# Small fp32 products of a hybrid decoder kernel issued to parts of the TensorE array

## The chip, the cores and the metric

The kernel runs on one core of one Trainium2 chip. The metric is the device time of one execution in microseconds (us). Each kernel is timed over several runs, and one further execution is recorded by the hardware profiler. PE is TensorE's multiplying side and PEld its weight-loading side, DVE is VectorE, ACT is ScalarE, POOL is GpSimd, and SP is the engine that here only issues DMAs.

## What is computed

The reference is a two-layer causal decoder trunk on 512 tokens of width 1024, all in float32. Cut to its frame:

```python
for layer in range(2):
    hn = _rmsnorm(h, norm_mix[layer])
    if layer == 0:
        proj = hn @ mix_w_in
        oa = _s5_mixer(proj[..., :512], ...)        # 32 groups of 16 channels, 64 complex states each
        ob = _hgrn2_mixer(proj[..., 512:], ...)     # 4 heads, chunked gated linear recurrence
        mix = concatenate([oa, ob], -1) @ mix_w_out
    else:
        mix = _dilated_attention(hn, positions, att_w_qkv, att_w_o)
    h = h + mix
    h = h + _conv_ffn(_rmsnorm(h, norm_ffn[layer]), ...)   # 1024 -> 2*2816, width-3 conv, gate, -> 1024
return _rmsnorm(h, norm_final)

# attention: 3 branches (dilation 1, 4, 16) x 8 heads of 64 dims, banded blocks of 128 queries
s = einsum('bdhnqe,bdhnke->bdhnqk', qb, kc)
o = einsum('bdhnqk,bdhnke->bdhnqe', exp(s - m), vc) / den      # then merged over the branches by their den
```

## The kernel before

Channels lie on the 128 partitions and the 512 tokens on the free axis. Every large product (projections, FFN, output projections) is made in three products of rounded parts: `mm3` (L183 to L187) multiplies the high and low parts of weights and activations into one PSUM bank of 512 columns. Weights stream from HBM in pieces of 1 MB, and ACT and DVE split each into `whi` and `wlo` (L124, L125). These products make up most of the program on TensorE. Between them stand many small products of plain fp32, whose operands are not split. In the trace each plain fp32 product stands as two weight loads and two matmuls, called two passes below.

The small products that the change touches are these:

- `rms_cols` (L258): the mean of squares of 128 tokens. The stationary operand is a 128x128 block of squares, the moving one a column of 1/1024. It runs four to eight times at each norm. For the attention's norm, four of the eight blocks take every fourth token (`"p (i r) -> p r i", r=4`).
- `s5_data` (L791, L811, L812): the S5 mixer in four feature tiles, 8 groups each. The first group of products takes 128x128 tables `gt` by 128x64 inputs `U`; then swap, multiplications and a scan on ACT, DVE and POOL make `X`; the second group adds `tz` by `U` and `ca` by `X` for each g. ACT copies the sum out (L814).
- `att_scores` (L1052, L1056): for a pair of heads e = 0, 1, which lie on partitions 0 to 63 and 64 to 127, blocks of 128 queries by 128 or 256 keys. Side 0 is the branch of dilation 1, with contiguous tokens. Side 1 is the two other branches, whose both operands take every fourth token.
- `att_merge` (L1140, L1142): probabilities, transposed to `pT`, by values, 64 columns of `v` for each head of the pair, into the banks `on` (side 0) and `oc` (side 1). Head e writes partitions 64e to 64e+63. DVE then multiplies both banks by the merge weights (L1146, L1147).

What else TensorE does between two large products is set by hand: `PROG` (L77) is text in which a dot stands for two or so large products and a letter for one step of a chain (`a`, `b`: S5; `h`, `k`: HGRN2; `s`: scores; `m`: merge). A chain's `yield` ends a step. A scheduler may move instructions a little, engine by engine; each engine then runs its own list in order.

Of the kernel before, what the change touches and what calls it, by code (L numbers as in the profile page):

```python
# [153 lines left out]
class Kernel:  # L154
# [94 lines left out]
    def rms_cols(self, blocks=(0, 1, 2, 3)):  # L249

        nc, ss = self.nc, self.ss
        u, n = blocks[0], len(blocks)
        pn = self.auxbank()
        parts = 1 if self.nsplit else 2
        for i in range(parts):
            for b in blocks:
                x = ss[i][:, 128 * b:128 * b + 128] if b < 4 else ss[i].rearrange("p (i r) -> p r i", r=4)[:, b - 4]
                nc.tensor.matmul(pn[:, b:b + 1], x, self.meanw, start=(i == 0 and b == u), stop=(i == parts - 1 and b == blocks[-1]))  # L258
        rc = self.xp.tile([128, 8], F32, name="rc")
        ms = self.xp.tile([128, 8], F32, name="ms")  # L260
        r = slice(u, u + n)
        nc.vector.tensor_scalar(ms[:, r], pn[:, r], EPS, None, op0=OP.add)
        self.rsqrt(rc[:, r], ms[:, r], self.xp, n)
        return rc
# [517 lines left out]
    def s5_data(self, ft, tables):  # L782
        nc = self.nc
        V, PL = nc.vector, nc.gpsimd
        gt, ca, tz, cs, sn, dec = tables
        U = self.U[ft]
        pa = self.auxbank()
        yield
        for g in range(8):
            o = slice(64 * g, 64 * g + 64)  # L790
            nc.tensor.matmul(pa[:, o], gt[:, g], U[:, g], start=True, stop=True)  # L791
        f = lambda ap: ap.rearrange("p g m -> p (g m)")
        z, t2, zs = self.tmp(), self.tmp(), self.tmp()
        self.swap(t2, pa)
        V.tensor_tensor(z, pa, f(cs), op=OP.mult)
        V.tensor_tensor(t2, t2, f(sn), op=OP.mult)
        V.tensor_tensor(z, z, t2, op=OP.add)
        V.tensor_tensor_scan(zs, f(dec), z, 0.0, op0=OP.mult, op1=OP.add)
        yield
        self.swap(t2, zs)  # L800
        X = self.tmp().rearrange("p (g m) -> p g m", g=8)
        PL.memset(X[:, :, 0:1], 0.0)
        z3 = lambda ap: ap.rearrange("p (g m) -> p g m", g=8)[:, :, 0:63]
        V.tensor_tensor(t2, t2, f(sn), op=OP.mult)
        PL.tensor_tensor(z, zs, f(cs), op=OP.mult)
        V.tensor_tensor(X[:, :, 1:64], z3(z), z3(t2), op=OP.subtract)
        yield
        py = self.auxbank()
        for g in range(8):
            o = py[:, 64 * g:64 * g + 64]  # L810
            nc.tensor.matmul(o, tz[:, g], U[:, g], start=True, stop=False)  # L811
            nc.tensor.matmul(o, ca[:, g, 2:10].rearrange("p d c -> p (d c)"), X[:, g], start=False, stop=True)  # L812
        ys = self.tmp()
        nc.scalar.activation(ys, py, AF.Copy)  # L814
        d = self.dr.tile([8, 128, 64], F32, name="yd")
        nc.scalar.dma_start(d.rearrange("i (c g) m -> (i c) (g m)", g=8), ys)
        yb = self.tmp()
        nc.scalar.dma_start(yb.rearrange("p (i m) -> p i m", i=8), d.rearrange("i p m -> p i m"))
        yield
        V.scalar_tensor_tensor(yb, self.u[:, ft], self.s5D[:, ft:ft + 1], yb, op0=OP.mult, op1=OP.add)  # L820
        nc.scalar.activation(self.u[:, ft], yb, AF.Gelu_apprx_tanh)
# [213 lines left out]
    def att_scores(self, side, pair):  # L1035


        nc, wk = self.nc, self.wk
        V, A, mm = nc.vector, nc.scalar, nc.tensor.matmul
        mx, st, qk = pair["mx"], pair["st"], pair["qk"]  # L1040
        k = 2 * side
        rows = [slice(64 * e, 64 * e + 64) for e in range(2)]
        p = [wk.tile([128, 4, 256], F32, name=f"p{side}", bufs=4) for e in range(2)]
        mask = self.mask[:, side:side + 2].rearrange("p a b -> p (a b)")
        for i in range(2):
            sc = [self.auxbank().rearrange("p (b n) -> p b n", b=2) for e in range(2)]
            for j in range(2):
                b = 2 * i + j
                c = 128 if side == 0 and b == 0 else 0
                for e, r in enumerate(rows):  # L1050
                    if side == 0:
                        mm(sc[e][:, j, c:], qk[0][r, 0, 128 * b:128 * b + 128], qk[0][r, 1, 128 * b - 128 + c:128 * b + 128], start=True, stop=True)  # L1052
                    else:
                        for g in (1, 2):
                            x = qk[g].rearrange("p a (i r) -> p a r i", r=4)
                            mm(sc[e][:, j, 128 * g - 128:128 * g], x[r, 0, b], x[r, 1, b], start=True, stop=True)  # L1056
            for e in range(2):
                for j in range(2):
                    b = 2 * i + j
                    c = 128 if side == 0 and b == 0 else 0  # L1060
                    V.tensor_tensor_reduce(p[e][:, b, c:], sc[e][:, j, c:], mask[:, c:], 1.0, NEG, OP.add, OP.max, accum_out=mx[:, e, b:b + 1])
                V.tensor_scalar(st[:, k, 2 * i:2 * i + 2, e], mx[:, e, 2 * i:2 * i + 2], -0.125, None, op0=OP.mult)
                for j in range(2):
                    b = 2 * i + j
                    c = 128 if side == 0 and b == 0 else 0
                    A.activation(p[e][:, b, c:], p[e][:, b, c:], AF.Exp, scale=0.125, bias=st[:, k, b, e:e + 1], accum_out=st[:, k, b, 2 + e:3 + e])
            if i == 0:
                yield
        for e in range(2):
            pair["p"][side, e] = p[e]  # L1070
        yield
# [42 lines left out]
    def att_merge(self, hp, pair):  # L1114
        nc, st = self.nc, pair["st"]
        V, mm = nc.vector, nc.tensor.matmul

        dc = self.dr.tile([T, 4], F32, name="dc")
        nc.sync.dma_start(dc.rearrange("(i r) n -> i r n", r=4), st[:, 2])
        nc.sync.dma_start(st[:, 1], dc.rearrange("(b p) n -> p b n", p=128))  # L1120
        yield
        pT = {}
        self.att_turn(pair, 1, 0, pT)
        yield
        W = self.att_weights(st)
        yield
        for side, e in ((0, 0), (1, 1), (0, 1)):
            self.att_turn(pair, side, e, pT)
            yield
        while None in [self.att_value(hp, g) for g in range(3)]:  # L1130
            yield
        vs = [self.att_value(hp, g) for g in range(3)]
        on, oc = self.auxbank(), self.auxbank()
        for e in range(2):
            s = slice(64 * e, 64 * e + 64)
            for b in range(4):
                hc = slice(128 * b, 128 * b + 128)
                todo = [j for j in range(2) if b or j]
                for j in todo:
                    mm(on[s, hc], vs[0][:, b - 1 + j, s], pT[0, e, b, j], start=(j == todo[0]), stop=(j == 1))  # L1140
                for j in range(2):
                    mm(oc[s, hc], vs[1 + j][:, b, s], pT[1, e, b, j], start=(j == 0), stop=(j == 1))  # L1142
            yield
        ot, o2 = (self.wk.tile([128, T], F32, name=n, bufs=1) for n in ("ot", "o2"))
        nat = lambda x: x.rearrange("p (i r) -> p r i", r=4)
        V.tensor_tensor(nat(o2), oc.rearrange("p (r i) -> p r i", r=4), nat(W[:, 1]), op=OP.mult)  # L1146
        V.tensor_tensor(ot, on, W[:, 0], op=OP.mult)  # L1147
        V.tensor_tensor(ot, ot, o2, op=OP.add)
        self.split(self.oh[:, hp], self.ol[:, hp], ot)
# [76 lines left out]
```

## Time and profile before

| | |
|---|---|
| median of 3 runs | 1317.2 us (1316.0 to 1318.52) |
| the profiled execution | 1316.5 us, span 1314.5 us |
| TensorE busy | 1271.3 us (97%), 6890 matmuls recorded |
| DVE busy | 821.9 us (63%) |
| ACT busy | 548.2 us (42%) |
| POOL busy | 144.4 us (11%) |
| mean granted TensorE clock | 0.988 |
| HBM traffic | 94 GB/s mean |

The span is the time between the first and the last instruction; the run's own time is 2.0 us longer. "Busy" is the share in which an engine has at least one instruction under way. Matmuls overlap one another in the array, so a matmul's recorded duration is longer than the step from one start to the next, and the steps are what adds up to time.

### The profile page before, as it was taken

The numbers are of one execution on the slowest core, as the hardware profiler recorded it, in microseconds if no ns is written. First come the engines' busy times: TensorE is split into PE (matmuls) and PEld (weight loads), VectorE is DVE, ScalarE is ACT, GpSimd is POOL, SyncE is SP. The second block draws the span as 40 slices with busy tenths as digits, with TensorE's granted clock in tenths as the row PEclk, the third lists the DMA queues.
The fourth block names the chain that finished last, engine by engine and source line by source line (L and its number), as shares of the span: only waits on it lengthen the run. The fifth ranks groups of instructions, "written<-read, shape, count | busy, mean of one in ns | idle before, by whom it ended". The sixth has DMA issues, their size and how long they took to land.

```text
span 1314.5 us, 17115 instructions
## 1 busy us (share of the span) xinstructions
PE 1271.3 (97%) x6890; PEld 1052.8 (80%) x6890; DVE 821.9 (63%) x1368; ACT 548.2 (42%) x867; POOL 144.4 (11%) x121
## 2 busy tenths in 40 slices
PE   7888999999999999999999999999899999999997
PEld 5677887878888888888888888898688888888886
DVE  7877688768777776333553535546777777773233
ACT  6457755335444444222334333424354444442221
POOL 2356111020000000001020101100300000000000
PEclk9989999999999999999999999999999999999998
DMA  6422122432223222222322322322122222222211
GB/s 208 136 69 77 49 81 59 136 101 94 96 96 100 97 97 96 96 97 96 109 82 92 94 96 73 94 81 81 62 97 98 100 96 96 96 96 96 97 64 65
DMA packets 36047, 123.19 MB, mean 94 GB/s; under 512 B 14912, under 2 KB 17536, under 8 KB 23296
## 3 DMA queue, kind: packets, MB, share of 16 engines
q1 hardware_dynamic: 22672, 113.32, 26.2%
q10 hardware_dynamic: 13296, 8.78, 2.3%
q8 instruction: 54, 0.88, 0.3%
q14 instruction: 25, 0.20, 0.1%
HBM read 116.26 MB, written 4.26 MB: 92 GB/s over the span
## 4 chain that ended last, share of the span: by engine, by line
PE 87%; DVE 8%; ACT 2%; issue 1%; POOL 1%; DMA 1%; ACTq 0%; DVEq 0%; SPq 0%; POOLq 0%
PE pt L185 26%; PE pt L187 26%; PE pt L186 26%; PE px L1056 1%; DVE wlo L125 1%; DVE xl L229 1%; PE px L1142 1%; PE px L1081 1%; PE px L1140 1%; PE px L812 1%; PE px L811 1%; PE px L517 1%; PE px L1052 1%; PE px L258 0%; DVE H L541 0%
## 5 line engine op out<-in xcount | busy, mean ns | idle before, releaser
L185 PE MATMUL pt<-xh,whi 128*128 128x512 f32 x1024 | 404.0, 395 | 8.9 <-ACT whi L124 7.1
L187 PE MATMUL pt<-xl,whi 128*128 128x512 f32 x1024 | 402.5, 393 | 2.3 <-DVE xl L229 2.3
L186 PE MATMUL pt<-xh,wlo 128*128 128x512 f32 x1024 | 401.9, 392 | 1.2 <-DVE wlo L125 1.2
L125 DVE TENSOR_TENSOR wlo<-stg,whi 128x1024 fp32r<-128x1024 f32 (+1 forms) x213 | 258.4, 1214 | 228.7 <-ACT whi L124 226.0
L124 ACT ACTIVATE whi<-stg 128x1024 fp32r<-128x1024 f32 (+1 forms) x213 | 215.7, 1013 | 261.7 <-PE pt L187 219.8
L185 PEld LDWEIGHTS pt<-xh,whi 128*128 128x128 f32 x1024 | 193.4, 189 | 51.7 <-ACT whi L124 7.5
L187 PEld LDWEIGHTS pt<-xl,whi 128*128 128x128 f32 x1024 | 193.7, 189 | 44.3 <-DVE xl L229 3.9
L186 PEld LDWEIGHTS pt<-xh,wlo 128*128 128x128 f32 x1024 | 193.9, 189 | 41.9 <-DVE wlo L125 2.3
L185 PE MATMUL pt<-ah,whi 128*128 128x512 f32 (+1 forms) x374 | 142.5, 381 | 0.0
L187 PE MATMUL pt<-al,whi 128*128 128x512 f32 (+1 forms) x374 | 141.7, 379 | 0.0
L186 PE MATMUL pt<-ah,wlo 128*128 128x512 f32 (+1 forms) x374 | 140.4, 375 | 0.0
L847 DVE TENSOR_TENSOR hu<-pt,rs 128x512 f32<-128x512 f32 x88 | 60.2, 688 | 62.8 <-PE pt L187 60.0
L187 PEld LDWEIGHTS pt<-al,whi 128*128 128x128 f32 x374 | 70.2, 188 | 14.5
L186 PEld LDWEIGHTS pt<-ah,wlo 128*128 128x128 f32 x374 | 70.2, 188 | 13.9
L185 PEld LDWEIGHTS pt<-ah,whi 128*128 128x128 f32 x374 | 70.3, 188 | 12.4
L848 ACT ACTIVATE b<-hu,cw 128x512 f32<-128x512 f32 x88 | 70.7, 808 | 5.0 <-DVE hu L847 4.4
L191 ACT ACTIVATE ah<-b 128x512 fp32r<-128x512 f32 x44 | 27.7, 630 | 107.3 <-DVE b L853 107.3
L237 POOL TENSOR_TENSOR ss<-H 128x512 f32<-128x512 f32 x4 | 4.5, 1135 | 595.0 <-DVE H L871 507.3
L850 DVE SCALAR_TENSOR_TENSOR b<-hu,cw,b 128x512 f32<-128x512 f32 x88 | 65.9, 751 | 2.7
L849 DVE SCALAR_TENSOR_TENSOR b<-hu,cw,b 128x512 f32<-128x512 f32 x88 | 65.5, 746 | 0.0
L852 ACT ACTIVATE b<-b 128x512 f32<-128x512 f32 x44 | 27.8, 632 | 72.9 <-DVE b L850 72.9
L185 PE MATMUL pt<-whi,xh 128*128 128x512 f32 x128 | 53.2, 415 | 0.0
(328 smaller groups left out, 1521.5 us busy)
## 6 DMA issues: line engine op xcount, KB each, us to landing
stg<-w_f SPq DMA_DIRECT2D x44, 1024.0 KB
stg<-w_g SPq DMA_DIRECT2D x22, 1024.0 KB
stg<-w_qkv SPq DMA_DIRECT2D x18, 1024.0 KB
stg<-w_mix SPq DMA_DIRECT2D x8, 1024.0 KB
H<-xT SPq DMA_DIRECT2D x8, 256.0 KB
stg<-w_moa SPq DMA_DIRECT2D x2, 1024.0 KB
b<-xT ACTq DMA_DIRECT2D x8, 256.0 KB
stg<-w_mob SPq DMA_DIRECT2D x2, 1024.0 KB
```

The costliest lines, as they stand in the source:

```text
L124: nc.scalar.activation(hi[:, c], s[:, c], AF.Copy)
L125: nc.vector.tensor_tensor(lo[:, c], s[:, c], hi[:, c].bitcast(F32), op=OP.subtract)
L185: mm(pt, sh, mh, start=first, stop=False)
L186: mm(pt, sl, mh, start=False, stop=False)
L187: mm(pt, sh, ml, start=False, stop=last)
L191: nc.scalar.activation(hi, x, AF.Copy)
L229: nc.vector.scalar_tensor_tensor(self.xl[:, i], x, g, self.xh[:, i].bitcast(F32), op0=OP.mult, op1=OP.subtract)
L847: V.tensor_tensor(x[:, 2:], pt, rs, op=OP.mult)
L848: nc.scalar.activation(y, x[:, 2:], AF.Identity, scale=cw[:, f, 2:3], bias=cw[:, f, 3:4])
L849: V.scalar_tensor_tensor(y, x[:, 1:T + 1], cw[:, f, 1:2], y, op0=OP.mult, op1=OP.add)
L850: V.scalar_tensor_tensor(y, x[:, 0:T], cw[:, f, 0:1], y, op0=OP.mult, op1=OP.add)
L852: nc.scalar.activation(half[0], half[0], AF.Silu)
```

## The change

Four kinds of small product are cut so that several of them occupy different parts of the array. The values of two heads (64 output columns each) alternate instead of one head following the other. A block of scores is cut into two halves of 64 queries, so that with the two heads there are four parts of 64 rows by 64 columns. The S5 products and the norms' column sums are cut into four parts of 32 output columns each. What is computed is the same, and the number of values multiplied too; there are more and smaller instructions. In `att_merge` the two steps now end after blocks 1 and 3 instead of after each head.

```diff
@@ rms_cols
-                nc.tensor.matmul(pn[:, b:b + 1], x, self.meanw, start=(i == 0 and b == u), ...)
+                for q in range(0, 128, 32):
+                    nc.tensor.matmul(pn[q:q + 32, b:b + 1], x[:, q:q + 32], self.meanw, start=(i == 0 and b == u), ...)
@@ s5_data
-            nc.tensor.matmul(pa[:, o], gt[:, g], U[:, g], start=True, stop=True)
+            for q in range(0, 128, 32):
+                nc.tensor.matmul(pa[q:q + 32, o], gt[:, g, q:q + 32], U[:, g], start=True, stop=True)
...
-            nc.tensor.matmul(o, tz[:, g], U[:, g], start=True, stop=False)
-            nc.tensor.matmul(o, ca[:, g, 2:10].rearrange("p d c -> p (d c)"), X[:, g], start=False, stop=True)
+            cx = ca[:, g, 2:10].rearrange("p d c -> p (d c)")
+            for y, z in ((tz[:, g], U[:, g]), (cx, X[:, g])):
+                for q in range(0, 128, 32):
+                    nc.tensor.matmul(py[q:q + 32, 64 * g:64 * g + 64], y[:, q:q + 32], z, start=(y is not cx), stop=(y is cx))
@@ att_scores
-                for e, r in enumerate(rows):
-                    if side == 0:
-                        mm(sc[e][:, j, c:], qk[0][r, 0, 128 * b:128 * b + 128], qk[0][r, 1, ...], start=True, stop=True)
-                    else:
-                        for g in (1, 2):
-                            mm(sc[e][:, j, 128 * g - 128:128 * g], x[r, 0, b], x[r, 1, b], start=True, stop=True)
+                for g in range(side, 2 * side + 1):
+                    for h in (slice(0, 64), slice(64, 128)):
+                        for e, r in enumerate(rows):
+                            if side == 0:
+                                mm(sc[e][h, j, c:], qk[0][r, 0, 128 * b:128 * b + 128][:, h], qk[0][r, 1, ...], start=True, stop=True)
+                            else:
+                                mm(sc[e][h, j, 128 * g - 128:128 * g], x[r, 0, b, h], x[r, 1, b], start=True, stop=True)
@@ att_merge
-        for e in range(2):
-            s = slice(64 * e, 64 * e + 64)
-            for b in range(4):
-                ...
-                    mm(on[s, hc], vs[0][:, b - 1 + j, s], pT[0, e, b, j], start=(j == todo[0]), stop=(j == 1))
-                    mm(oc[s, hc], vs[1 + j][:, b, s], pT[1, e, b, j], start=(j == 0), stop=(j == 1))
-            yield
+        for b in range(4):
+            todo = [(on, 0, j, vs[0][:, b - 1 + j]) for j in range(2) if b or j] + [(oc, 1, j, vs[1 + j][:, b]) for j in range(2)]
+            for po, side, j, v in todo:
+                for e in range(2):
+                    s = slice(64 * e, 64 * e + 64)
+                    mm(po[s, hc], v[:, s], pT[side, e, b, j], start=(j == 0 or side == 0 and b == 0), stop=(j == 1))
+            if b % 2:
+                yield
```

Three places show how the instructions stand on TensorE. A row gives line, operation, the tile written, the tiles read, output partitions by moving columns, and a count. The first is the values of the first pair of heads, head 0 before (its step is followed by head 1 later), where px_6165 is `on` and px_6166 is `oc`:

```order
L1140 MATMUL px_6165<-pT_5839,v0_5590 64x128
L1142 MATMUL px_6166<-pT_5701,va_6096 64x128 x2
L1140 MATMUL px_6165<-pT_5839,v0_5590 64x128 x2
L1142 MATMUL px_6166<-pT_5701,va_6096 64x128 x2
L1140 MATMUL px_6165<-pT_5839,v0_5590 64x128
L1140 MATMUL px_6165<-pT_5846,v0_5590 64x128
```

The same place after the change, where px_6549 is `on` and px_6550 is `oc`, and pT_6207 and pT_6061 belong to head 0, pT_6390 and pT_6250 to head 1:

```order
L1144 MATMUL px_6549<-pT_6207,v0_5946 64x128
L1144 MATMUL px_6549<-pT_6390,v0_5946 64x128
L1144 MATMUL px_6550<-pT_6061,va_6480 64x128
L1144 MATMUL px_6550<-pT_6250,va_6480 64x128
L1144 MATMUL px_6550<-pT_6061,va_6480 64x128
L1144 MATMUL px_6550<-pT_6250,va_6480 64x128
```

Each product of head 0 now has the same product of head 1 behind it, in the other half of the output partitions; the count of 30 products a pair of heads stays.

The second place is the S5 mixer's second group of products for the first feature tile, before:

```order
L187 MATMUL pt<-wlo,xh 128x512
L811 MATMUL px<-U_428,tz_313 128x64
L185 MATMUL pt<-whi,xh 128x512
L812 MATMUL px<-b,ca_311 128x64
L811 MATMUL px<-U_428,tz_313 128x64
```

And after:

```order
L187 MATMUL pt<-wlo,xh 128x512
L815 MATMUL px<-U_440,tz_325 32x64 x4
L185 MATMUL pt<-whi,xh 128x512
L815 MATMUL px<-b,ca_323 32x64 x4
L815 MATMUL px<-U_440,tz_325 32x64 x4
```

Four products of 32 output partitions stand in the place of each one, and as before a single large product stands between the first of them and the rest of the group. Elsewhere the scheduler's list differs by shifts of a few places; on SP two loads of `w_qkv` weights stand earlier among the small transfers of the attention.

The third place is the first block of scores of side 1 (px are the banks of the two heads), before:

```order
L1056 MATMUL px_5368<-qkT_5167 128x128
L1056 MATMUL px_5369<-qkT_5167 128x128
L1056 MATMUL px_5388<-qkT_5167 128x128
L1056 MATMUL px_5389<-qkT_5167 128x128
L185 MATMUL pt_5347<-xh_4436,whi_5343 128x512
```

And after:

```order
L1060 MATMUL px_5704<-qkT_5479 64x128
L1060 MATMUL px_5705<-qkT_5479 64x128
L1060 MATMUL px_5704<-qkT_5479 64x128
L1060 MATMUL px_5705<-qkT_5479 64x128
L1060 MATMUL px_5732<-qkT_5479 64x128
```

The halves of the queries follow each other, each with both heads, so that four products in a row have four different pairs of row half and column half.

## Rows read from the trace of the kernel before

**Rows 1.** The page, part 1: busy us, share of the span, instructions.
```profile
PE 1271.3 (97%) x6890; PEld 1052.8 (80%) x6890; DVE 821.9 (63%) x1368; ACT 548.2 (42%) x867; POOL 144.4 (11%) x121
```

**Rows 2.** The page, part 4: the chain that ended last, shares by engine.
```profile
PE 87%; DVE 8%; ACT 2%; issue 1%; POOL 1%; DMA 1%; ACTq 0%; DVEq 0%; SPq 0%; POOLq 0%
```

**Rows 3.** Busy us by stretch; last columns: granted clock, DMA share, GB/s.
```profile
40.00:230.00 190.00, 171.90 (x1762) 140.01 (x1761) 146.79 (x281) 112.15 (x208) 66.75 (x58) 0.96 0.26 80
667.00:925.00 258.00, 257.24 (x1364) 219.55 (x1363) 133.39 (x284) 94.60 (x216) 27.14 (x11) 1.00 0.28 84
```

**Rows 4.** Groups by line and shape on PE: busy us, mean ns, idle before.
```profile
L1056 PE MATMUL px<-qkT 64*128 64x128 f32 x128 | 19.8, 448 | 0.0
L1140 PE MATMUL px<-pT,v 128*64 128x128 f32 x112 | 17.4, 276 | 0.6 <-DVE mx L1061 0.6
...
L812 PE MATMUL px<-b,ca 128*128 128x64 f32 x64 | 14.3, 311 | 2.4 <-DVE b L806 2.4
...
L1142 PE MATMUL px<-pT,va 128*64 128x128 f32 x64 | 9.3, 273 | 0.0
L1142 PE MATMUL px<-pT,vb 128*64 128x128 f32 x64 | 9.0, 273 | 0.0
```

**Rows 5.** Timeline of PE at the seam of two heads' values (start, length).
```profile
919.65 0.60 PE L1140 MATMUL px<-pT,v 128*64 128x128 f32 x4
920.08 0.27 PE L1142 MATMUL px<-pT,vb 128*64 128x128 f32 x1
920.09 0.32 PE L1140 MATMUL px<-pT,v 128*64 128x128 f32 x1
...
920.30 0.66 PE L1142 MATMUL px<-pT,vb 128*64 128x128 f32 x6
```

**Rows 6.** Timeline of PE in an S5 burst at full clock.
```profile
111.10 0.39 PE L812 MATMUL px<-b,ca 128*128 128x64 f32 x2
111.32 0.39 PE L811 MATMUL px<-U,tz 128*128 128x64 f32 x2
```

**Rows 7.** Timeline of PE around products already cut into 32 columns.
```profile
58.80 0.40 PE L187 MATMUL pt<-xl,whi 128*128 128x512 f32 x1
59.12 1.12 PE L757 MATMUL px<-ca,bb 128*32 128x128 f32 x32
60.17 0.50 PE L185 MATMUL pt<-xh,whi 128*128 128x512 f32 x1
```

**Rows 8.** Timeline of PE in the smallest products, bursts back to back.
```profile
204.50 0.45 PE L517 MATMUL px<-H 128*32 128x16 f32 x32
204.78 0.46 PE L509 MATMUL px<-hb 128*32 128x32 f32 x31
```

**Rows 9.** Groups by line and shape on PEld: loads of score blocks.
```profile
L1056 PEld LDWEIGHTS px<-qkT 64*128 64x128 f32 x128 | 16.9, 323 | 3.1 <-issue 2.2 <-DVE qkT L1032 0.6 <-PE pt L186 0.4
...
L1052 PEld LDWEIGHTS px<-qkT 64*128 64x128 f32 x64 | 4.8, 186 | 2.6 <-issue 2.3 <-DVE H L961 0.2
```

**Rows 10.** Timeline of PE: a burst of scores of side 1.
```profile
813.30 3.37 PE L1056 MATMUL px<-qkT 64*128 64x128 f32 x24
```

**Rows 11.** Timeline of PE: the attention norm's column sums.
```profile
640.91 2.81 PE L258 MATMUL px<-cst,ss 128*128 128x1 f32 x16
```

**Rows 12.** Busy us by stretch, columns as in rows 3.
```profile
81.70:91.90 10.20, 10.20 (x100) 9.21 (x101) 5.50 (x13) 4.28 (x8) 7.88 (x4) 0.50 0.27 112
...
644.90:648.30 3.40, 3.40 (x10) 2.63 (x9) 2.66 (x8) 1.55 (x2) 0.00 (x0) 0.50 0.00 0
```

**Rows 13.** Waits of all engines from 78 to 232 us (total, times, longest).
```profile
ACT b L814 <- PE px L812: 19.7, 4, 7.4
...
DVE H L540 <- PE px L517: 6.4, 6, 2.8
```

**Rows 14.** Timeline of PE in the first S5 burst.
```profile
82.48 0.63 PE L812 MATMUL px<-b,ca 128*128 128x64 f32 x2
82.91 0.63 PE L811 MATMUL px<-U,tz 128*128 128x64 f32 x2
```

More of the change, by code (lines that the diff above doesn't have):

```diff
@@ L257, in rms_cols @@
                 x = ss[i][:, 128 * b:128 * b + 128] if b < 4 else ss[i].rearrange("p (i r) -> p r i", r=4)[:, b - 4]
-                nc.tensor.matmul(pn[:, b:b + 1], x, self.meanw, start=(i == 0 and b == u), stop=(i == parts - 1 and b == blocks[-1]))
+                for q in range(0, 128, 32):
+                    nc.tensor.matmul(pn[q:q + 32, b:b + 1], x[:, q:q + 32], self.meanw, start=(i == 0 and b == u), stop=(i == parts - 1 and b == blocks[-1]))
         rc = self.xp.tile([128, 8], F32, name="rc")
@@ L809, in s5_data @@
         for g in range(8):
-            o = py[:, 64 * g:64 * g + 64]
-            nc.tensor.matmul(o, tz[:, g], U[:, g], start=True, stop=False)
-            nc.tensor.matmul(o, ca[:, g, 2:10].rearrange("p d c -> p (d c)"), X[:, g], start=False, stop=True)
+            cx = ca[:, g, 2:10].rearrange("p d c -> p (d c)")
+            for y, z in ((tz[:, g], U[:, g]), (cx, X[:, g])):
+                for q in range(0, 128, 32):
+                    nc.tensor.matmul(py[q:q + 32, 64 * g:64 * g + 64], y[:, q:q + 32], z, start=(y is not cx), stop=(y is cx))
         ys = self.tmp()
@@ L1049, in att_scores @@
                 c = 128 if side == 0 and b == 0 else 0
-                for e, r in enumerate(rows):
-                    if side == 0:
-                        mm(sc[e][:, j, c:], qk[0][r, 0, 128 * b:128 * b + 128], qk[0][r, 1, 128 * b - 128 + c:128 * b + 128], start=True, stop=True)
-                    else:
-                        for g in (1, 2):
-                            x = qk[g].rearrange("p a (i r) -> p a r i", r=4)
-                            mm(sc[e][:, j, 128 * g - 128:128 * g], x[r, 0, b], x[r, 1, b], start=True, stop=True)
+                for g in range(side, 2 * side + 1):
+                    for h in (slice(0, 64), slice(64, 128)):
+                        for e, r in enumerate(rows):
+                            if side == 0:
+                                mm(sc[e][h, j, c:], qk[0][r, 0, 128 * b:128 * b + 128][:, h], qk[0][r, 1, 128 * b - 128 + c:128 * b + 128], start=True, stop=True)
+                            else:
+                                x = qk[g].rearrange("p a (i r) -> p a r i", r=4)
+                                mm(sc[e][h, j, 128 * g - 128:128 * g], x[r, 0, b, h], x[r, 1, b], start=True, stop=True)
             for e in range(2):
@@ L1133, in att_merge @@
         on, oc = self.auxbank(), self.auxbank()
-        for e in range(2):
-            s = slice(64 * e, 64 * e + 64)
-            for b in range(4):
-                hc = slice(128 * b, 128 * b + 128)
-                todo = [j for j in range(2) if b or j]
-                for j in todo:
-                    mm(on[s, hc], vs[0][:, b - 1 + j, s], pT[0, e, b, j], start=(j == todo[0]), stop=(j == 1))
-                for j in range(2):
-                    mm(oc[s, hc], vs[1 + j][:, b, s], pT[1, e, b, j], start=(j == 0), stop=(j == 1))
-            yield
+        for b in range(4):
+            hc = slice(128 * b, 128 * b + 128)
+            todo = [(on, 0, j, vs[0][:, b - 1 + j]) for j in range(2) if b or j] + [(oc, 1, j, vs[1 + j][:, b]) for j in range(2)]
[5 more added lines that the diff above has]
+                yield
         ot, o2 = (self.wk.tile([128, T], F32, name=n, bufs=1) for n in ("ot", "o2"))
```

## The prediction, on record before the result

> **What bounds the kernel now.** Start with the busy shares: TensorE is at 97% and every other engine far below [rows 1]. Recorded matmuls overlap, so this alone does not make TensorE the bound; the chain of waits does: 87% of what ended last is PE [rows 2]. Then go by stretch, since the change touches three. In the attention, 667 to 925 us, PE is busy for 257.24 of 258.00 us and DVE for 133 [rows 3]: whatever TensorE saves there comes off the end. In the S5 and HGRN2 stretch, 40 to 230 us, PE is busy for 171.90 of 190 us and DVE for 147 [rows 3], so 18 us are TensorE's waits, L812's for DVE among them [rows 4]; a saving there can turn into a longer wait. The norms' sums stand inside or just before long runs of large products.
>
> The durations of single matmuls can't be added up; starts can. In a run of values, four passes (two products) step from 919.65 to 920.08, 0.43 us, 0.109 us each, though each is recorded as 0.27 [rows 4, 5]. All prices below are such steps.
>
> **Values.** Counts in [rows 4]: 112 + 64 + 64 = 240 passes, 240 x 0.109 = 26.2 us. A pass loads 64 columns and streams 128; half of the output columns is unused. Whether two heads can stream at once is seen where head 1's products start before head 0's have ended: at 920.08 a pass of L1142 starts and at 920.09, 0.01 us later, one of L1140 into the other half of the partitions; from then on both go on side by side [rows 5]. With the heads alternating throughout, the passes should pair: 13.1 us. Three such seams exist already, worth some 0.3 us each, so the saving is 26.2 - 13.1 - 0.9 = 12.2 us. Bounds: nothing (no pairing outside the seam) and 13.1. I take 12.2, since the seam is this very operation.
>
> **S5 products.** A pass of L811 or L812 takes 0.112 us (0.22 for two, at full clock) [rows 6]. It streams only 64 columns, about half of the values' 128, so its time is that of loading 128 columns. Cut to 32 columns, the load shrinks to a quarter and the stream of 64 columns is left: by proportion with the values 0.055 us. Four parts at a time are in the trace: 32 passes of L757, 32 columns each and 128 moving, take 1.12 us with a tail of 0.27, so 0.027 us a pass, a quarter of 0.109 [rows 7]. So four quarter passes take 0.055 us in place of one whole pass of 0.112. Per feature tile L791 has 16 passes and L811 with L812 have 32 (L812: 64 passes in four tiles [rows 4], the other two lines as many). L791: 64 x 0.112 = 7.2 becomes 3.6. The second group is 96 passes at 0.112 in three bursts, 10.8, which becomes 5.4; in the first burst a pass takes 0.213 (0.43 for two [rows 14]), since the granted clock was 0.50, the level of 1.2 GHz, from 81.70 to 91.90 [rows 12]: 32 x 0.213 = 6.8 becomes 3.4. Gross: 3.6 + 5.4 + 3.4 = 12.4 us.
>
> Against that, going from large products to a part of the array and back costs: L187 to L757 is 0.32 us where two large products step by 0.23, and the way back is longer too (60.17 is 0.20 after the last pass, which started 0.27 before 60.24) [rows 7]. That is 0.09 + 0.1, say 0.19 a visit. Whole products pay none. There are four L791 visits and, since the first product of each second group stands apart, eight others: 12 x 0.19 = 2.3 us. Net 10.1.
>
> How much reaches the end? In this stretch DVE and ACT also wait for TensorE: ACT 19.7 us for the end of the second groups, DVE 6.4 for L517 behind them [rows 13]. The waits go both ways, so most of the gain passes, but PE's own waits for DVE swallow some: I take 7 us, with 2 and 11 as bounds (all but the half-clock burst swallowed; all passed, with the clock back sooner).
>
> **Norm sums.** The 16 passes at 640.91 take 2.81 us [rows 11]. Four parts of 32 columns run in the shortest steps of the trace: 32 passes from 204.50 to 204.78, 0.009 us each [rows 8]. 64 quarter passes are then 0.6 us, twice that for the half with strided loads, so about 0.8 with the rest, plus 0.2 for the visit: 1.5 saved. The other visits have eight passes or four; at the same rates three save about 0.35 each and those at the end 0.2 together. Sum 2.7; bounds 0 and 4.
>
> **Clock after the attention norm.** From 644.90 to 648.30 the granted clock was 0.50 [rows 12], and what stood ahead was this burst with one moving column. At 1.2 GHz the large products do half the work, so 1.7 us are lost. With the burst down to about 1.2 us this may not happen; I count 1.5, bounds 0 and 1.7.
>
> **Scores.** Two heads already share the array by rows. A pair of passes of side 1 takes 0.25 us (24 passes in 3.37 us with a tail of 0.41 [rows 10]). Its load takes 323 ns against 186 for contiguous tokens [rows 9], and the load is halved. But the moving operand takes every fourth token too, and its matmuls are recorded longer than those of the values with as many moving columns, 448 against 276 [rows 4], so the stream is probably as slow as the load and is not cut. Bounds: half of 64 x 0.25, 8 us saved; or nothing, and more if four strided streams hinder each other. I take 1 us, near nothing. Side 0 streams 256 contiguous columns against a load of 128: the stream bounds it, nothing saved.
>
> One rule speaks against the S5 and norm parts. The smallest products in this trace step by 0.009 us [rows 8], so many small ones in the place of one need not cost more than it. The Trainium skill, TensorEngine Tiling (Array Packing), Instruction Overhead, says that a matmul has about 60 cycles of overhead, that one of one column takes as long as one of 60, and that a dimension already small should not be tiled; by it the sum would lose most of S5 and norms, and [rows 8] do not bear it out.
>
> **No new waits.** The same instructions of DVE and ACT wait for the same banks; `on` and `oc` were both complete only after head 1 and are now both complete after block 3. On SP a weight load moves ahead of two small transfers; if its buffer is late these go late, hidden as long as the large products that stand between scores and merge cover them.
>
> **Sum.** 12.2 + 7 + 2.7 + 1.5 + 1 = 24.4 us. The profiled execution took 1316.5 us (span 1314.5 and 2.0 around it), 0.7 under the median of 1317.2; against the median, 1317.2 - 24.4 = 1292.8, so 1293 us.
>
> **Rivals.**
> 1. *S5's gain turns into waits.* PE already waits 18 us there [rows 3], POOL and DVE set when `X` comes. If only 2 of 7 us pass, and the low clock stays, 1293 + 5 + 1.5 = about 1300. For it: DVE is busy for 147 of 190 us. Against: 19.7 us of ACT's waits end at the S5 products [rows 13]. Chance 0.12.
> 2. *A floor under each small pass.* If a pass with a real stream could not step faster than L757's 0.027 us [rows 7], 768 S5 quarter passes would take 20.7 us against 24.8 now, and less the visits 2 would be left of 10; a norm's four quarter passes would cost 0.11, no less than a whole one. Then 7 becomes about 2, and 2.7 + 1.5 become 0: 1293 + 9 = 1302. Against: [rows 8] step by 0.009 with 16 to 32 moving columns. Chance 0.07. The Trainium skill, TensorE: Matmul & The Clock Gate, Part 1, states such a floor, about 25 ns from start to start however few the columns.
> 3. *Four 64x64 parts run two at a time.* No row shows parts by rows and columns at once. If two heads' halves take turns, side 1 takes 64 x 0.25 = 16 us more and side 0, 32 pairs of at most 0.22, about 6 more: 1293 + 1 + 22 = 1316, no change. Chance 0.05.
> 4. *Slower:* the same, with one part at a time. The 16 + 6 us then come three times, 66 us: 1360. The point from which it decides is just under two parts at a time, where scores lose 24 us. For it: both halves read the same keys from the same partitions. Against: four parts of L757 each read their own moving columns on all partitions [rows 7]. Chance 0.04.
>
> What is left, 0.72, is the forecast, with its own range of 1286 to 1299.
>
> **Numbers.** A measurement here tells 0.2% from no change, so 1314.6 to 1319.8 is "same". Faster: 0.72 + 0.12 + 0.07 = 0.91; same 0.05; slower 0.04. The range takes in the forecast, both milder rivals and strided streams that hinder each other by half (8 us): 1285 to 1305.
>
> **What the next profile would show.** Values: starts of two heads' passes within 0.01 us of each other, 0.055 us a pass. S5: 64 passes of L791's successor in about 0.9 us. Norm: the burst at about 1.2 us, and no half clock behind it. Scores: the side 1 bursts as long as now within a tenth. The attention stretch some 14 us shorter, the FFN stretches unchanged but for their norm. I would be wrong if a score burst is longer than 3.37 us for the same blocks, if small passes step by 0.027 or more, or if PE's waits in the S5 stretch grow from 18 to over 23 us.

## The result, and the profile after

The changed kernel takes 1300.43 us (median of 4 runs, 1299.64 to 1302.15) where the kernel before took 1316.6 (1314.18 to 1318.52): a ratio of 0.988, with a 95% interval of 0.986 to 0.990. The profiled execution took 1300.12 us with a span of 1298.1 us. The forecast was 1293 with a range of 1285 to 1305: the direction and the range held, and about a third of the forecast gain did not come.

The page of the changed kernel, parts 1 and 4 (columns as in [rows 1, 2]):

```profile
PE 1245.3 (96%) x7826; PEld 1018.5 (78%) x7826; DVE 821.2 (63%) x1368; ACT 547.7 (42%) x867; POOL 146.9 (11%) x121
...
PE 81%; DVE 10%; ACT 3%; issue 3%; POOL 2%; DMA 1%; SPq 0%; DVEq 0%; ACTq 0%; POOLq 0%
```

TensorE is busy for 26 us less, but the span is only 16 us shorter: PE's share of the chain fell from 87% to 81%, and DVE's rose from 8% to 10%. The timeline of PE in the changed kernel shows the operations themselves, in the order of time: S5's first group, one wait, S5's second group, the attention norm, scores, values:

```profile
62.99 1.10 PE L793 MATMUL px<-U,gt 128*32 128x64 f32 x64
...
104.48 0.63 PE L518 MATMUL px<-H 128*32 128x16 f32 x32 [6.86 <-DVE H L542]
...
109.40 0.29 PE L815 MATMUL px<-U,tz 128*32 128x64 f32 x8
109.51 0.29 PE L815 MATMUL px<-b,ca 128*32 128x64 f32 x8
...
639.19 0.94 PE L259 MATMUL px<-cst,ss 128*32 128x1 f32 x64
803.71 3.04 PE L1060 MATMUL px<-qkT 64*64 64x128 f32 x48
...
842.56 0.61 PE L1144 MATMUL px<-pT,va 128*64 128x128 f32 x8
...
843.00 0.39 PE L1144 MATMUL px<-pT,v 128*64 128x128 f32 x4
```

Read by starts, eight passes of values take 843.00 - 842.56 = 0.44 us, 0.055 each where [rows 5] had 0.109. Eight quarter passes of S5 take 0.11 us (109.40 to 109.51), 0.014 each, so four take 0.055 where a whole pass took 0.112 [rows 6]. The attention norm's 64 quarter passes take 0.94 us as recorded, where 16 whole ones took 2.81 [rows 11]. A burst of scores of side 1 takes 3.04 us for what took 3.37 [rows 10].

The stretches of [rows 3] and [rows 12] in the changed kernel, and four more of its stretches (columns as in [rows 3]):

```profile
40.00:230.00 190.00, 164.81 (x2340) 128.81 (x2339) 147.39 (x274) 111.63 (x213) 67.98 (x57) 0.95 0.25 79
667.00:925.00 258.00, 254.69 (x1585) 211.24 (x1584) 145.12 (x301) 101.41 (x227) 32.18 (x19) 0.99 0.28 84
...
97.60:104.40 6.80, 0.01 (x1) 0.00 (x0) 5.67 (x8) 5.33 (x8) 3.60 (x5) 0.85 0.32 133
102.30:109.10 6.80, 4.62 (x117) 3.65 (x121) 5.75 (x8) 3.79 (x6) 5.95 (x5) 0.50 0.01 2
...
639.00:648.00 9.00, 8.66 (x100) 6.91 (x99) 7.37 (x22) 3.82 (x7) 0.00 (x0) 1.00 0.18 51
911.30:914.70 3.40, 3.40 (x9) 2.64 (x8) 2.27 (x4) 1.98 (x4) 1.26 (x2) 0.50 0.00 0
```

Behind the attention norm the clock is now whole (1.00 from 639 to 648). But in the S5 and HGRN2 stretch PE stands for 190 - 164.81 = 25.2 us where it stood for 18.1 [rows 3], and 6.8 us at half clock (1.2 GHz) have appeared at 102.30, 3.4 at 911.30. The 10.2 us at half from 81.70 [rows 12] have become 3.4, from 81.9 to 85.3. The longest waits of PE in the first of these stretches (total, times, longest), of the changed kernel:

```profile
PE px L518 <- DVE H L542: 8.2, 4, 6.9
PE px L750 <- DVE g L729: 5.7, 3, 4.2
PE px L815 <- DVE b L808: 3.6, 2, 3.0
```

In the kernel before, PE waited for the same instruction (L541 there) ahead of the same product (L517 there) 1.7 us in all. These are that product and that instruction, before:

```profile
105.56 0.45 PE L517 MATMUL px<-H 128*32 128x16 f32 x32 [1.68 <-DVE H L541]
...
104.21 1.29 DVE L541 TENSOR_TENSOR H<-H 128x256 f32<-128x256 f32 x1
```

The list of DVE ahead of the long wait, in the changed kernel, with PE idle from 97.6 to 104.48:

```profile
96.88 0.68 DVE L797 TENSOR_TENSOR b<-px,cs 128x512 f32<-128x512 f32 x1
97.48 0.68 DVE L798 TENSOR_TENSOR b<-b,sn 128x512 f32<-128x512 f32 x1
98.08 0.74 DVE L823 SCALAR_TENSOR_TENSOR b<-u,s5D,b 128x512 f32<-128x512 f32 x1
98.74 0.68 DVE L799 TENSOR_TENSOR b<-b 128x512 f32<-128x512 f32 x1
99.46 1.22 DVE L800 TENSOR_TENSOR_SCAN b<-dec,b 128x512 f32<-128x512 f32 x1
100.60 0.40 DVE L541 TENSOR_TENSOR H<-H 128x256 f32<-128x256 f32 x1
102.09 1.13 DVE L806 TENSOR_TENSOR b<-b,sn 128x512 f32<-128x512 f32 x1 [1.09 <-ACT b L781]
103.14 1.28 DVE L542 TENSOR_TENSOR H<-H 128x256 f32<-128x256 f32 x1
```

From 97.6 to 104.4 DVE is busy for 5.67 of 6.8 us, mostly with the S5 chain's arithmetic, and waits 1.09 us in it for ACT; the one multiplication that HGRN2 waits for (L542) stands last. In the kernel before the same instruction began at 104.21, here at 103.14. The whole stretch starts 1.9 us earlier in this profile, though (the first norm is at 26.5 us, before at 28.4), so counted from there DVE's list ends 0.8 us later than it did, and not sooner, although the S5 products became shorter. The lists are not quite the same: L806 stands ahead of L542 here, where a split of weights stood before. In a second profile of the changed kernel the longest such wait is 7.7 us, with the S5 part alone 7.0, and in the two profiles of the changed kernel with whole S5 products 1.6 and 1.9.

**A ledger by stretches.** Lengths in us between starts of named PE instructions, each read from the timeline of one profiled execution. A: first norm to the end of HGRN2's last transposes. B: attention norm to the first score. C: first score to the product behind the last value pass. D: from there to the FFN norm. "Half" is the time at half clock within A. The kernels are those of the experiments below; "2nd" is a second profile of the same kernel.

| kernel | A | half in A | B | C | D |
|---|---|---|---|---|---|
| before | 213.2 | 17.1 | 26.7 | 255.9 | 32.6 |
| after | 213.7 | 20.5 | 23.9 | 242.5 | 34.9 |
| after, 2nd | 214.1 | 23.9 | 23.9 | 242.5 | 33.6 |
| values alone | 213.8 | 17.1 | 26.7 | 245.1 | 32.6 |
| S5 alone | 210.4 | 13.7 | 25.1 | 255.9 | 35.2 |
| norms alone | 211.0 | 17.1 | 23.9 | 255.9 | 32.7 |
| scores alone | 213.1 | 17.1 | 26.7 | 253.6 | 32.6 |
| after, S5 whole | 210.6 | 13.7 | 23.9 | 242.7 | 35.2 |
| after, S5 whole, 2nd | 212.0 | 13.7 | 23.9 | 242.7 | 32.7 |
| after, filled | 209.9 | 10.2 | 23.9 | 242.5 | 32.7 |
| light, S5 whole | 209.3 | 17.1 | 25.2 | 255.9 | 35.2 |
| light, S5 in parts | 202.8 | 13.7 | 26.7 | 255.9 | 32.6 |

C repeats to 0.3 us in kernels with the same scores and values, and B with the same norms, but for S5 alone and the light kernel with whole S5 products, where no half clock stood behind the attention norm; A and D do not. In A the S5 part gives nothing in the changed kernel; in D all kernels with 35 us have a half clock in it, 3.4 or 6.8 us long, and those with 32.6 or 32.7 have none. What lies outside the table changes little with the parts: the time up to the first norm is 25.4 to 28.5 us in these profiles, whichever part is in, so 1.9 of the 16.4 us between the spans of before and after are not the change's; the time between A and B and from the FFN norm on is shorter with the norms' part by 0.2 to 0.3 and 0.8 to 1.2 us.

### The profile page after: what moved, and what is told of

Its sections match the earlier page's. It is cut to its first block, busy times and chain, and to the rows that moved or that the text cites. A ratio compares the mean times of both kernels' runs of the same rounds, so it can differ in the third digit from the quotient of the medians.

```text
span 1298.1 us, 18995 instructions
## 1 busy us (share of the span) xinstructions
PE 1245.3 (96%) x7826; PEld 1018.5 (78%) x7826; DVE 821.2 (63%) x1368; ACT 547.7 (42%) x867; POOL 146.9 (11%) x121
## 3 DMA queue, kind: packets, MB, share of 16 engines
q1 hardware_dynamic: 22672, 113.32, 26.5%
## 4 chain that ended last, share of the span: by engine, by line
PE 81%; DVE 10%; ACT 3%; issue 3%; POOL 2%; DMA 1%; SPq 0%; DVEq 0%; ACTq 0%; POOLq 0%
PE pt L185 25%; PE pt L187 25%; PE pt L186 25%; DVE wlo L125 2%; PE px L1060 1%; DVE xl L229 1%; PE px L1085 1%; ACT tz L763 1%; PE px L1144 1%; PE px L1057 0%; POOL g L728 0%; PE px L560 0%; PE px L558 0%; DMA H<-xT 0%; DMA wrow<-wd 0%
```

## The experiments

**Each part alone**, on one chip, against 23 runs of the kernel before (median 1315.47 us). Each is the kernel before with one piece of the diff shown above, and the other three left as they were.

```diff
@@ values alone
-        for e in range(2):
-            for b in range(4):
+        for b in range(4):
...
+                for e in range(2):
+                    mm(po[s, hc], v[:, s], pT[side, e, b, j], ...)
@@ S5 alone (both groups)
-            nc.tensor.matmul(pa[:, o], gt[:, g], U[:, g], start=True, stop=True)
+            for q in range(0, 128, 32):
+                nc.tensor.matmul(pa[q:q + 32, o], gt[:, g, q:q + 32], U[:, g], start=True, stop=True)
...
@@ norms alone
-                nc.tensor.matmul(pn[:, b:b + 1], x, self.meanw, ...)
+                for q in range(0, 128, 32):
+                    nc.tensor.matmul(pn[q:q + 32, b:b + 1], x[:, q:q + 32], self.meanw, ...)
@@ scores alone
...
+                    for h in (slice(0, 64), slice(64, 128)):
+                        for e, r in enumerate(rows):
...
+                                mm(sc[e][h, j, 128 * g - 128:128 * g], x[r, 0, b, h], x[r, 1, b], start=True, stop=True)
```

Expected of the values: 

> The kernel before with the values' part of the change alone. In the traces the steps of the values take 25.8 us before and 14.2 after, so 11.6 us are saved on TensorE. Theory (the last pair's saving is spent waiting for its merge weights, whose DMA lands late): the fourth pair's 3 us are mostly lost, 9 us faster, and DVE waits for the DMA of wrow before the last merge. Rival (the wait for wrow comes only from the other parts or from chance): 11.6 us faster.

Expected of S5: 

> The kernel before with the S5 part alone. The passes step by 0.014 us instead of 0.11, some 7 us less of TensorE's time. Theory (DVE's own list from 80 to 106 us and its chains afterwards set the end of this stretch): within 2 us of the kernel before, and PE's wait for DVE ahead of a small HGRN2 product (L518) is 5 us longer. Rival, the prediction's step: 7 us of it pass, 7 us faster, and the loss in the full change lies elsewhere.

Expected of the norms: 

> The kernel before with the norms' column sums alone. Theory: the three bursts of 8 passes and the one of 16 save 0.35 + 0.35 + 1.7 + 0.35 us, and the half clock behind the attention norm does not occur, 1.7 us more: 4 us faster. Rival (the clock drop is not tied to that burst, or waits take the rest): 2 us faster or less.

Expected of the scores: 

> The kernel before with the scores' part alone. Theory from the steps in the two traces (26.8 us before, 24.1 after): 2.7 us faster, side 1 giving 2.3 of it. Rival, the prediction's step: 1 us faster or nothing, the 2.7 being lost again in waits of DVE, which reads the scores.

| kernel | median us (runs) | ratio, 95% interval | gain by it | clock | span x clock |
|---|---|---|---|---|---|
| before | 1315.47 (23) | | | 0.988 | 1297.2 |
| values alone | 1303.79 (6) | 0.9905 (0.9884 to 0.9925) | 12.5 | 0.9895 | 1287.5 |
| S5 alone | 1314.55 (12) | 0.9992 (0.998 to 1.0005) | 1.1 | 0.988 | 1296.2 |
| norms alone | 1307.95 (6) | 0.9943 (0.9921 to 0.9964) | 7.5 | 0.992 | 1295.0 |
| scores alone | 1311.49 (12) | 0.9963 (0.9945 to 0.998) | 4.9 | 0.9895 | 1295.4 |

Of the expectations, S5's theory came true, with PE's longest wait for DVE at 7.0 us; of the values the rival did, since DVE waited for PE and not for the transfer. The norms and the scores gave more time than either of their theories.

A gain is 1315.47 x (1 - ratio). The four sum to 26.0 us, where the change as a whole gave 0.012 x 1316.6 = 15.8: in time, the parts don't add. The last two columns say why. "Clock" is the median over the runs of the mean granted clock. "Span x clock", the median of each run's product, is an estimate of the span had the clock never been at half. It counts half of every microsecond at half clock as lost, also where PE waits or has little left to do (in every profile 5.0 to 8.4 us of it lie behind the last norm's column sums, at the end of the kernel), so it takes too much for the clock. By it the gains are 9.7, 1.0, 2.2 and 1.8, together 14.7, and the changed kernel (1282.8, from the four runs of the result) has 14.4 less than the 1297.2 of before. In the later runs below it has 1281.3 where before has 1297.7, 16.4 less. So at full clock the parts add, to within some 2 us. What differs is the clock's share, span x (1 - clock): 15.8 us before, 13.7, 15.8, 10.4 and 13.8 with one part each, and 15.6 with all four. The norms alone, for one, have a whole clock where [rows 12] had 0.50; this is a stretch of that kernel behind its attention norm:

```profile
640.00:644.00 4.00, 3.68 (x17) 2.75 (x16) 3.67 (x13) 1.64 (x3) 0.00 (x0) 1.00 0.22 35
```

So with the norms alone 5.4 us of clock are won besides their 2.2, and the full change has them no more. Of the 5.4 only some 1.7 stand behind the attention norm; the rest, by the profiles of the two kernels, is less half clock ahead of the first norm and behind the last. The clock has three digits in each run, so such a product is good to some 0.7 us.

**The change without its S5 part**, and **the last pair without its own merge weights**, with the two **light** kernels on one chip (before: 1317.0 us, 12 runs, clock 0.987).

```diff
@@ without S5's part, from after (both groups)
-            for q in range(0, 128, 32):
-                nc.tensor.matmul(pa[q:q + 32, o], gt[:, g, q:q + 32], U[:, g], start=True, stop=True)
+            nc.tensor.matmul(pa[:, o], gt[:, g], U[:, g], start=True, stop=True)
...
@@ last pair with the weights of the pair before, from after
+        if hp == 3:
+            return self.W_last
         px, ws, W = self.auxbank(), ...
...
+        self.W_last = W
```

Expected without S5's part: 

> The changed kernel with the S5 products given back to the whole array; values, norms and scores stay in parts. Alone, the four parts gave 12.5, 7.5, 4.9 and 1.1 us, together 26, where all four in one kernel gave 16. Theory (the S5 part saves its passes and gives them back: PE waits for DVE's list at L517, and with shorter bursts its clock is at half for longer; in the changed kernel 20.4 us at half before the attention, in the kernel with the values alone 17.0): the S5 part is worth nothing or less in the full change, so this kernel is as fast or faster: 1294 to 1300 us. If the parts simply added, it would take 1316.6 less 12.5, 7.5 and 4.9, 1291.7. Rival (the S5 part does give its 7 us, and something else is lost): 1305 to 1308.

It took 1296.0 us (1294.14 to 1297.4, 4 runs), ratio 0.9844 (0.9825 to 0.9864), clock 0.990: less than the full change (1300.43 us, then on other runs of before). The theory holds, and the gain that the forecast gave to S5 is not there.

Expected of reused weights: 

> The changed kernel, with the last pair of heads taking the merge weights of the pair before, so that the weights' two transfers (to wd and back to wrow) and the transpose ahead of them fall away for that pair; this part of the computation is left out. Theory (the end of the attention is late by DVE's wait for wrow, 1.5 us more idle of PE ahead of the output projection than in the kernel with the values alone, and by the 3.4 us at half clock that follow): FFN1's norm begins 1.5 to 3.2 us sooner after the last value pass, 32.6 us instead of 34.9, and the time is 1297 to 1299 us. Rival (the wait lies beside other work, and the loss is the clock alone, which falls wherever it falls): 34 to 35 us and 1299.5 to 1301.

It took 1299.15 us (1298.74 to 1299.52), ratio 0.9869 (0.9852 to 0.9886), clock 0.988. The wait that it removes is this one, first the changed kernel's, then the same instruction with the values alone:

```profile
907.17 1.09 DVE L1149 TENSOR_TENSOR o<-px,wrow 128x512 f32<-128x512 f32 x1 [4.92 <-DMA wrow<-wd]
```

```profile
910.96 1.09 DVE L1145 TENSOR_TENSOR o<-px,wrow 128x512 f32<-128x512 f32 x1 [3.41 <-PE px L1140]
```

In the changed kernel the transfer lands after the last value pass, which ends at 905.6; with the values alone DVE starts as soon as that pass has ended. Without the transfer stretch D is still 35.1 us, since 6.8 us at half clock lie in it. So of D's 2.3 us the transfer is at most a part, and the rival is nearer: 1299.15 lies between the two. In a second profile of the changed kernel (below) the same wait was 4.39 us and D 33.6 with no half clock in it, so the transfer costs about 1 us when it comes late and the clock up to 2.6 when it falls there.

The light kernels leave out DVE's multiplications by the level factors in HGRN2, so their output is not the reference's:

```diff
@@ light, from before and from S5 alone
-                V.tensor_tensor(half(Q)[:, :, 1], half(Q)[:, :, 1], Bc(Fv[:, :, 0:1]), op=OP.mult)
-                V.tensor_tensor(half(k)[:, :, 0], half(k)[:, :, 0], Bc(Fv[:, :, 1:2]), op=OP.mult)
```

Expected of the whole S5 products: 

> The kernel before, without the two multiplications by the level factors of each level of the HGRN stage on DVE (L540 and L541, some 34 us of DVE in 31 pairs of instructions); that part of the computation is left out. It is the base for the kernel beside it. Both theories: the HGRN stretch gets shorter, since PE's products of the levels wait for these, by 5 to 25 us: 1290 to 1311.

Expected of S5 in parts: 

> The kernel with the S5 products alone in parts, without the same multiplications (left out as in the kernel beside it). Theory (S5's gain is hidden by DVE's list in the HGRN stretch: with DVE light it comes out): at least 4 us faster than the kernel beside it, up to the 7 of the prediction's term. Rival (the gain is lost to the clock, or to the S5 chain's own steps on DVE, ACT and GpSimd, which are left as they are): within 2 us of the kernel beside it, as 1.1 us with DVE's full list.

With whole products it took 1313.68 us (1308.51 to 1319.54, 9 runs), above the 1290 to 1311 that both theories gave it: with whole S5 products, DVE's multiplications hold the kernel up by only some 3 us (before: 1317.0). With S5 in parts it took 1304.87 (1303.41 to 1305.84, 4 runs): 8.8 us less, where the same cut gives 1.1 with DVE's full list. By span x clock it is 1294.6 against 1289.5, 5.1 us against 1.0; the other 3.7 are the clock's (0.988 and 0.990). The ledger has the gain where the products are: A is 6.5 us shorter, with 3.4 less at half. So DVE's list does hide the S5 part's gain, about 4 us of it. What still holds PE up in the light kernel is the S5 chain itself, as the waits of PE from 60 to 245 us show:

```profile
PE px L812 <- DVE b L805: 7.0, 2, 5.0
PE px L747 <- DVE g L726: 5.3, 2, 2.9
```

**The clock in the wait**, with the changed kernel and the one without S5's part again, all on one chip (before: 1316.34 us, 9 runs).

```diff
@@ filled, from after, in the loop over the levels of a head
+            if l == 2 and h == 0:
+                for _ in range(28):
+                    mm(p1[:, 448:512], self.ident, self.ident[:, 0:64], start=True, stop=True)
```

Expected of the changed kernel: 

> The changed kernel once more, on one chip with the two kernels beside it. Theory (a shorter S5 stretch of PE becomes a wait, and the clock is lower in it): 1299 to 1302, mean granted clock 0.988, as at first.

Expected without S5's part: 

> The changed kernel with whole S5 products, on the same chip as the changed kernel. Theory (the S5 part gives about 1 us at full clock and costs 3 us of clock in the HGRN stretch): 2 to 5 us less than the changed kernel beside it, at a clock of 0.990. Rival (the two differed by their chips alone): within 1 us of it, at the same clock.

Expected of the filled kernel: 

> The changed kernel with 28 further fp32 products of 128x128 by 64 columns, whose result nobody reads, ahead of the products of the third level of the first HGRN2 head, where PE waits 6.9 us for DVE and the clock is then at half for 6.8 us. They take 28 x 0.224 = 6.3 us, which fits into the wait. Theory (the clock falls because PE stood still there): no half clock from 102 to 109 us, 3.4 us less than the changed kernel beside it, less up to 1.5 for starting the last of them late. Rival (the clock falls for something else, or falls later instead): the time of the changed kernel or up to 1.5 us more.

| kernel | median us (runs) | ratio, 95% interval | clock | span x clock |
|---|---|---|---|---|
| after | 1299.74 (5) | 0.9882 (0.986 to 0.9904) | 0.988 | 1281.3 |
| after, S5 whole | 1295.08 (5) | 0.9849 (0.9828 to 0.9871) | 0.990 | 1281.5 |
| after, filled | 1295.29 (4) | 0.9844 (0.9826 to 0.9863) | 0.992 | 1282.8 |

The changed kernel came as expected, and the kernel with S5 whole is 4.7 us below it. Over both sets, nine runs each, all runs of the changed kernel but one are above every run with S5 whole. By span x clock the two are level (0.2 us apart, with runs that spread over 4 to 5): the S5 part gains nothing here and costs by the clock. The filled kernel does more work than the changed one and is 4.5 us faster, more than the 3.4 of its theory. Its timeline of PE, and then its stretches with the filling products and behind them:

```profile
97.37 6.36 PE L516 MATMUL px<-cst 128*128 128x64 f32 x56
105.58 0.63 PE L521 MATMUL px<-H 128*32 128x16 f32 x32 [1.84 <-DVE H L545]
```

```profile
97.40:103.70 6.30, 6.30 (x57) 6.19 (x55) 5.01 (x9) 3.70 (x6) 1.84 (x2) 1.00 0.56 182
105.00:108.40 3.40, 2.83 (x37) 2.35 (x38) 3.40 (x4) 1.49 (x2) 3.28 (x4) 0.55 0.00 0
```

PE still waits for L545 until 105.58, at the end for 1.84 us, so nothing is gained in the wait itself. What is gained is clock: 3.4 us at half behind it in place of 6.8, 10.2 in all of stretch A in place of 20.5 and 23.9, and over the runs 0.992 in place of 0.988. A is 3.8 and 4.2 us shorter than in the two profiles of the changed kernel. Half of the time at half clock that is gone would be 5.1 and 6.8, so not all of that time had cost anything. The theory had none left behind the wait; half of it stayed. That the filling moves the clock elsewhere in A and D too (D is 32.7, with no half clock) was not foreseen by either. The Trainium skill, TensorE: Matmul & The Clock Gate, Part 1, says that the throttled clock is the array's default, and that activity releases it. This pair of kernels agrees: 6.3 us more of products in a wait, and 0.992 in place of 0.988.

## Why the forecast was nearly right, and too low

**Values: the mechanism right, the term a little large.** Two heads' passes do run side by side at 0.055 us a pass. The term was 12.2; the bursts on PE became 11.6 us shorter in all (25.8 to 14.2), the stretch C alone 10.8, and span x clock 9.7. A burst of 60 passes still has its entry and exit from the large products, and the last one is now split: two passes, a large product and then the other 58.

**S5: this step failed.** The forecast's price held: 0.055 us for four quarter passes; L793's 64 took 1.10 with their tail. S5's bursts on PE, each up to the next other product, take 17.0 us where they took 24.0, and 14.7 with the S5 part alone, so 7.0 to 9.3 of the 10.1 were there to be had. The step "most of the gain passes", 7 of 10.1 us, did not hold: 1.0 us passes at full clock. The forecast weighed ACT's and DVE's waits for PE as a sign that a faster PE would release them. ACT's wait for the second groups did fall, from 19.7 to 14.6 us, but on DVE stood its own list, which ended no sooner than before, and PE now waits for it at L518. This is the first half of rival 1, whose 2 us were nearer than 7. Its time, 1300, was what came, but partly by luck: its other half, that the low clock behind the attention norm stays, did not come, and half clock elsewhere made up for it. The chance given to it was 0.12. The forecast's own bound for it ("PE's waits grow from 18 to over 23") was passed at 25.2. The Trainium skill, TensorEngine Tiling (Array Packing), PSUM Bottleneck, warns that after a fourfold speedup of TensorE the copies out of PSUM may become the bottleneck. Here PE's long wait ends not with the copy (L817) but with DVE's arithmetic (L542).

**Norms: the size right, the reason for the clock only in part.** Stretch B is 2.9 us shorter, of the 1.5 for the attention norm's own passes and 1.5 of clock that the terms gave it, and behind it the clock is whole. By span x clock all norms give 2.2 of the 2.7. The forecast took the burst with one moving column as what stood ahead of the half clock. None of the seven profiles with the short burst has a half clock behind it, but of the six with the long one two have none either, S5 alone and the light kernel with whole products. This is S5 alone behind its burst of 2.81 us:

```profile
638.00:645.00 7.00, 7.00 (x32) 5.70 (x33) 5.52 (x18) 2.51 (x4) 0.00 (x0) 1.00 0.13 28
```

There B is 25.1 us: by it 1.6 of the 2.9 are clock and 1.3 the passes. So the 1.5 of clock was a chance taken and not a sure gain.

**The clock as a whole: the step that was missing.** The forecast counted 1.5 us of it at one place and took the rest as it was. It falls at several places, for up to 15.8 us in all, and in each kernel at others. In the changed kernel 6.8 us at half begin within the wait of 6.9 us at L518, and A has 20.5 and 23.9 us at half where it had 17.1 before. S5 alone has the same wait with 6.8 us at half beside it and yet only 13.7 in A, so the wait alone does not tell the sum.

**Scores: small, as said, a little better.** C is 2.3 us shorter with the scores alone, where 1 was counted: the burst of 24 passes went from 3.37 to 3.04 us. So cutting them into four parts, with strided streams, made no burst longer.

**No new waits: wrong in one place.** The paragraph looked at SP's loads, but not at the transfer of the merge weights of the last pair. With values twice as fast, DVE can wait for it: 1 to 1.5 us in two profiles of the changed kernel, and not in the four of other versions with the same values and transfers. In the two late ones SP issues the read back (`wrow`) 3.6 and 3.1 us behind the write to `wd`, in the others 1.4, and only in the late ones a 16 KB instruction transfer starts between the two. That this holds the write up is not shown.

**The floor (rival 2) and the parts that take turns (rivals 3 and 4)** did not come: S5's quarter passes step by 0.014 us, half of L757's 0.027 [rows 7], and scores got faster. By the Trainium skill's issue floor of about 25 ns (TensorE: Matmul & The Clock Gate, Part 1) the eight quarter passes from 109.40 to 109.51 would take 0.2 us, by estimate. The trace has 0.11.

**Open** is where in A and D the clock falls: the changed kernel had 20.5 and 23.9 us at half in A in two profiles, and no run here fixes the places one by one. That the S5 part's loss is clock rests on clock and time over 14 runs of three kernels on one chip, not on a single fall that was taken away whole.

**The version that beats before and after** is either of two: the change without its S5 part, 1296.0 and 1295.1 us on two chips, or the change with the wait filled, 1295.3.

## What to carry over

A burst on the bounding engine that becomes shorter is worth its steps only where nothing else ends just behind it: take the other engines' lists up to the next instruction that both need, and see when each ends without the burst. If the engine then stands still, its clock can cost more than the burst had saved. Compare parts by span times granted clock as well as by time: here the first added up to within 2 us and the second missed by 10. And before cutting products into parts of the array, see what waits on both sides: where PE went on with other products (values, scores, norms) the saving arrived, between dependent steps (S5) it did not.

## What was not expected of the hardware

- Work that nobody reads made the kernel 4.5 us faster: 6.3 us of extra products in a wait of 6.9 us raised the mean granted clock from 0.988 to 0.992.
- Small passes go on getting cheaper well below the large ones' price: 0.014 us for 32 columns by 64 moving, and 64 passes of 32 columns by one take 0.94 us with the tail.
- The two transfers of 256 KB from `wd` to `wrow` had landed when the last value pass ended in four profiles with the new values, and landed after it in both profiles of the changed kernel: DVE's wait was 4.92 and 4.39 us where it was 3.4.
